# One 25-way switch for every two experts in place of a five-way switch for each expert

## The chip, the cores and the metric

The kernel runs on one core of a Trainium2 chip. Its engines are TensorE (PE, with its weight loads as PEld), VectorE (DVE), ScalarE (ACT), GpSimd (POOL) and SyncE (SP), which here issues nearly all DMAs. Each engine has its own program and its own sequencer. The metric is the time of one execution on the device in microseconds (us), as the median of several runs; a profile of one execution explains it.

## The reference

A trunk of two layers over 256 latent tokens and 256 context tokens of width 1024. Layer 0 is a bidirectional RWKV-7 mixer and a dense SwiGLU; layer 1 is a pooling mixer and a top-2-of-8 expert SwiGLU. All is in fp32. The change touches the last part alone:

```python
def swiglu(h, w1, w3, w2):
    return (jax.nn.silu(h @ w1) * (h @ w3)) @ w2

def moe_swiglu(h, router_w, router_b, w1, w3, w2):
    logits = (h @ router_w).astype(jnp.float32) + router_b.astype(jnp.float32)
    top_logit, top_idx = lax.top_k(logits, TOP_K)
    top_p = jax.nn.softmax(top_logit, axis=-1)
    gates = jnp.einsum('btk,btke->bte', top_p,
                       jax.nn.one_hot(top_idx, N_EXPERTS, dtype=jnp.float32)).astype(h.dtype)
    y = jnp.zeros_like(h)
    for e in range(N_EXPERTS):
        y = y + gates[..., e:e + 1] * swiglu(h, w1[e], w3[e], w2[e])
    return y
```

256 tokens with two experts each are 512 rows of work over 8 experts. How many rows an expert gets is known only at run time.

## The kernel before

The expert stage is the last third of the kernel. The router (L1617 to L1640) makes, on VectorE with small matmuls, `sel` (which token takes which expert), `posm` (the position of a token among the rows of an expert) and `pc` (the rows of each expert). L1643 to L1648 compare `pc` with the four bounds 32, 64, 128, 192 and write `cnt`, one whole number from 0 to 4 for each expert. `values_load` (L1697) loads these numbers into registers of TensorE, VectorE, ScalarE and SyncE (`ARM_ENGINES`).

L1931 is the loop over the eight experts. For each expert, POOL writes the one-hot matrix `oh` of the next expert (L1657), and then the four engines enter a switch with five arms, each on its own, by one computed branch. The profile gives the instructions of the switch itself to L2071 (moves, register operations, `COMPARE_BRANCH`) and L1934 (a prefetch hint for the way out, the first instruction of an arm). At the end of an arm another branch leads back to the common path. The arms differ by the blocks of rows that they work on:

- `[Full, Full]` over 192 rows, `[Full, Small]` from 129 to 192, `[Full]` from 65 to 128, `[Small]` from 33 to 64, `[Tiny]` up to 32.
- `Full` splits each weight into two parts (ScalarE L1284 `wh`, VectorE L1285 `wl`) and multiplies in three passes (L237). `Small` and `Tiny` take the weights as they are (L1786 and L1800; L1751 and L1769), with column groups of TensorE for several pieces at once.

`arm(e, kinds)` (L1858) goes through one expert in a fixed order of 13 steps, "u0 u1 u2 d0 u3 d1 ... t5 d4 d5": u is the up product, t a turn (L1763 in Tiny, L1832 in Full), d the down product. In the step t5 it already gathers the tokens of the next expert: `gather(oh, xgs[0])` (TensorE L1666, then VectorE L1653 and ScalarE L1652 write `xg`), `halves()` splits them (L1674, L1675), `turn_oh` turns the one-hot (L1681). At the end of the arm VectorE writes the expert's output rows to `yf` (L1775 in Tiny, L1850 in Full). The next expert's arm adds them to the sum: `scatter` (TensorE L1724, VectorE L1726). A Full arm does this scatter first of all, a Tiny or Small one after its step u1.

The weights come in 17 pieces of an expert, mostly 1 MB each, over SyncE's queue (L1536). 19 slots in SBUF hold them; when a step has used a piece, SyncE starts the load of the piece 19 further on in the same slot.

Instructions within one straight block are put in order by a scheduler that may move work of a later step ahead; between the blocks of a switch nothing moves. POOL is not part of the switch.

Of the kernel before, what the change touches and what calls it, by code (L numbers as in the profile page):

```python
# [8 lines left out]
F32 = mybir.dt.float32  # L9
F32R = mybir.dt.float32r  # L10
I32 = mybir.dt.int32
AF = mybir.ActivationFunctionType
ALU = mybir.AluOpType
# [4 lines left out]
P = 128  # L18
# [7 lines left out]
NE = 8  # L26
BOUNDS = (32, 64, 128, 192)
# [71 lines left out]
class Sched:  # L99
# [12 lines left out]
    def op(self, tag, fn, deps=(), acq=(), use=(), at=0.0, nbytes=0, dur=None):  # L112
        o = Op()
        o.tag, o.fn, o.acq, o.nbytes = tag, fn, list(acq), nbytes
        o.eng, us, rank = WORK[tag]
        o.dur, o.prio = us if dur is None else dur, at + rank
        for t in acq:
            t.by = o
        deps = [d for d in deps if d is not None] + [t.by for t in use if t.by is not o]
        o.wait, o.ready, o.end, o.next, o.seq, o.names = len(deps), 0.0, None, [], len(self.ops), None  # L120
        for d in deps:
            d.next.append(o)
        for t in list(acq) + list(use):
            t.users.append(o)
        self.ops.append(o)
        return o
# [74 lines left out]
def kernel(ctx: ExitStack, tc: tile.TileContext, I: dict, out: bass.AP, dbg=None):  # L201
    nc = tc.nc
# [55 lines left out]
    def ada_copy(ps):  # L258
        nc.vector.tensor_copy(ab, ps[:, 0:256])

    def ada_turn(pt):
        for j in range(2):
            nc.tensor.transpose(pt[:, P * j:P * j + P], ab[:, P * j:P * j + P], ident)
# [331 lines left out]
    S = Sched()  # L595
# [9 lines left out]
    def tok(n):  # L605
        return rings[n].tok()
# [7 lines left out]
    def pb(t):  # L614
        return PB[t.i + (2 if t.ring is rings["gen"] else 0)]
# [35 lines left out]
    for q in range(4):  # L651
# [7 lines left out]
        for h in range(2):  # L659
# [6 lines left out]
            a = op("v_hi", v_hi, deps=[ld], acq=[sp[h]], use=[rw], at=-1.5 + 0.5 * q)  # L666
# [12 lines left out]
        for tp in range(2):  # L679
# [8 lines left out]
            a = op("v_out", v_out, deps=prev[2 * tp:2 * tp + 2] + [opened], acq=[vt], use=[accs[tp]], at=-1.5 + 0.5 * q)  # L688
# [6 lines left out]
    for n, (l, w) in enumerate(todo[ada_at[0]:]):  # L695
# [14 lines left out]
        a = op("ada_copy", lambda: ada_copy(ADAB), deps=mms + ada_done[-1:], use=[bt], at=pr)  # L710
        g = tok("gen")
        t = op("ada_turn", lambda g=g: ada_turn(pb(g)), deps=[a], acq=[g], at=pr)
# [553 lines left out]
    c2p = ctx.enter_context(tc.tile_pool(name="c2p", bufs=1, reuse_waits="tile"))  # L1266
# [54 lines left out]
    def C2(n, a=0, b=None):  # L1321
        o, w = CONST2[n]
        return consts2[:, o - POOLED + a:o - POOLED + (w if b is None else b)]
# [206 lines left out]
    def piece(g):  # L1530
        sh = pieces[g][1]
        return slots[g % NS][:, 0:math.prod(sh[1:])].rearrange("p (a b) -> p a b", a=sh[1])
# [70 lines left out]
    exp_p = ctx.enter_context(tc.tile_pool(name="exp_p", bufs=1, reuse_waits="tile"))  # L1603
# [31 lines left out]
    pp, pc = gen(), gen()  # L1635
    pe(nc.tensor.matmul(pp[:, 0:16], lhsT=C2("tri"), rhs=sel.rearrange("p t e -> p (t e)"), start=True, stop=False))
    pe(nc.tensor.matmul(pp[:, 8:16], lhsT=C2("ones"), rhs=sel[:, 0], start=False, stop=True))
    for t in range(2):
        pe(nc.tensor.matmul(pc[:, 0:8], lhsT=C2("ones"), rhs=sel[:, t], start=(t == 0), stop=(t == 1)))
    nc.vector.scalar_tensor_tensor(posm, sel, -1000.0, pp[:, 0:16].rearrange("p (t e) -> p t e", t=2),  # L1640
                                   op0=ALU.mult, op1=ALU.add)

    cnt = c2p.tile([P, NE], I32, name="cnt")  # L1643
    armf = c2p.tile([P, NE], F32, name="armf")
    S.chain(nc.vector.tensor_scalar(armf, pc[:, 0:8], float(BOUNDS[0]), None, op0=ALU.is_le))
    for i, b in enumerate(BOUNDS[1:]):
        S.chain(nc.vector.scalar_tensor_tensor(armf if i + 2 < len(BOUNDS) else cnt, pc[:, 0:8], float(b), armf,
                                               op0=ALU.is_le, op1=ALU.add))  # L1648
    ENG = mybir.EngineType
    def affine3(dt, dst, src):  # L1650
        if dt % 2:
            return nc.scalar.activation(dst, src, AF.Identity, scale=r_a[:, dt:dt + 1], bias=r_b[:, dt:dt + 1])  # L1652
        return nc.vector.tensor_scalar(dst, src, r_a[:, dt:dt + 1], r_b[:, dt:dt + 1], op0=ALU.mult, op1=ALU.add)  # L1653

    def onehot(e, b, eng, oh):
        for t in range(2):
            eng.tensor_scalar(oh[:, t], C2("iota", P * b, P * b + P), posm[:, t, e:e + 1], None, op0=ALU.is_equal)  # L1657

    def gather(oh, xg, n=P):

        for d4 in range(2):
            pt = gen()
            for j in range(4):
                dt = 4 * d4 + j
                for t in range(2):
                    nc.tensor.matmul(pt[:, P * j:P * j + n], lhsT=z[:, t, P * dt:P * dt + P], rhs=oh[:, t, 0:n], start=(t == 0), stop=(t == 1))  # L1666
            for j in range(4):
                affine3(4 * d4 + j, xg[:, 4 * d4 + j], pt[:, P * j:P * j + n])
# [8 lines left out]
    def turn_oh(oh, ohT):  # L1677

        po = gen()
        for t in range(2):  # L1680
            nc.tensor.transpose(po[:, P * t:P * t + P], oh[:, t], ident)  # L1681
        nc.scalar.activation(ohT, po[:, 0:256].rearrange("p (t s) -> p t s", t=2), AF.Copy)
# [4 lines left out]
    spare = sct.rearrange("p d c -> p (d c)")  # L1687
# [2 lines left out]
    xs3 = [exp_p.tile([P, DT, P], F32R, name="xs" + n) for n in "hl"]  # L1690
    yf = exp_p.tile([P, D], F32, name="yf")
    nc.gpsimd.memset(yf, 0.0)
    oh, ohB = exp_p.tile([P, 2, P], F32, name="oh"), spare.rearrange("p (t s) -> p t s", t=2)
    xgs = [exp_p.tile([P, DT, P], F32, name="xg"), None]
    ohT = [consts[:, 2 * P:4 * P].rearrange("p (t s) -> p t s", t=2), C2("tri", 0, 2 * P).rearrange("p (t s) -> p t s", t=2)]
    ARM_ENGINES = (ENG.PE, ENG.DVE, ENG.Activation, ENG.SP)
    vals = [nc.values_load(cnt[0:1, e:e + 1], engines=ARM_ENGINES, min_val=0, max_val=len(BOUNDS)) for e in range(NE)]  # L1697
    onehot(0, 0, nc.vector, oh)
    gather(oh, xgs[0])
    turn_oh(oh, ohT[0])  # L1700
    halves()
    ex, p1_, sm = rt("ex", [P, 2, 1]), rt("p1_", [P, 2, 1]), rt("sm", [P, 2, 1])
    nc.vector.tensor_tensor(ex, m2, m1, op=ALU.subtract)
# [148 lines left out]
    def rows_of(v):  # L1852
        return lambda k: v[k // v[0].shape[1]][:, k % v[0].shape[1]]
# [4 lines left out]
    def arm(e, kinds):  # L1858
        full, two, end = kinds[0] is Full, len(kinds) > 1, e == NE - 1
        if full and e > 0:  # L1860
            scatter(e - 1, ohT[(e - 1) % 2])
        if two:
            onehot(e, 1, nc.vector, ohB)
            n = P if kinds[1] is Full else 64
            xgs[1] = yf[:, 0:DT * n].rearrange("p (d s) -> p d s", d=DT)
            gather(ohB, xgs[1], n)
            turn_oh(ohB, ohT[(e + 1) % 2])
        w, at, g = {}, {}, 17 * e
        for a, c in acts:
            if a != "t":  # L1870
                at[a, c] = range(g, g + (2 if a == "u" and c < 5 else 1))
                g = at[a, c][-1] + 1
                w[a, c] = [piece(i) for i in at[a, c]]
                if a == "d":
                    w[a, c] = w[a, c][0]
                else:
                    w[a, c] = rows_of(w[a, c])
        bl = [k(w, xgs[b], b, accb[2 * ((e + b) % 2):2 * ((e + b) % 2) + 2]) for b, k in enumerate(kinds)]
        ups, dns = {}, {}
        eats = list(at)  # L1880

        def split(i):

            if not full or i >= len(eats):
                return
            a, c = eats[i]
            if a == "u":
                v = [piece(g) for g in at[a, c]]
                ups[c] = parts_of([split_weight(t) for t in v], v[0].shape[1])
            else:  # L1890
                dns[c] = split_weight(w["d", c])

        split(0)
        for a, c in acts:
            if a != "t":
                split(eats.index((a, c)) + 1)
            for k in bl[::-1]:
                if a == "u":
                    k.up(c, ups)
                elif a == "d":  # L1900
                    k.down(c, dns)
                else:
                    k.turn(c)
            if a == "u":
                for k in bl[::-1]:
                    if c > 0:
                        k.turn(c - 1)
                    k.act(c)
            if (a, c) == ("u", 1) and e > 0 and not full:
                scatter(e - 1, ohT[(e - 1) % 2])  # L1910
            if a == "t" and not end:
                gather(oh, xgs[0])
                halves()
                if not two:
                    turn_oh(oh, ohT[(e + 1) % 2])
            for i in at.get((a, c), ()):
                pload(i + NS)
        if two:
            bl[1].end()
            scatter(e, ohT[(e + 1) % 2])  # L1920
            if not end:
                turn_oh(oh, ohT[(e + 1) % 2])
        bl[0].end()

    ARMS = [[Full, Full], [Full, Small], [Full], [Small], [Tiny]]

    extra = ctx.enter_context(tc.tile_pool(name="extra", bufs=1, reuse_waits="tile"))
    for g in range(EXTRA):
        slots.append(extra.tile([P, 2048], F32, name=f"slot{MORE + g}"))
        pload(len(slots) - 1)  # L1930
    for e in range(NE):  # L1931
        if e + 1 < NE:
            onehot(e + 1, 0, nc.gpsimd, oh)
        for k in tc.Switch({g: vals[e] for g in ARM_ENGINES}, len(ARMS)):  # L1934
            arm(e, ARMS[k])
    scatter(NE - 1, ohT[(NE - 1) % 2])
    rg, rb = (piece(17 * NE + i)[:, 0] for i in range(2))
    z = zx.tile([P, 2, D], F32, tag="z", name="z4")
# [136 lines left out]
```

## Time and profile before

| | before |
|---|---|
| median of 3 runs (lowest to highest) | 1416.85 us (1416.37 to 1421.95) |
| profiled execution, its time | 1420.72 us |
| its span, first to last instruction | 1418.9 us |
| granted clock of TensorE, mean | 0.889 |
| busy: PE, DVE, ACT, POOL | 81%, 65%, 44%, 24% of the span |
| expert stage | about 943 to 1403 us |
| HBM read | 273.17 MB |

A row of the chain of waits has a start, a length and the engine, DMA or "issue" that the chain went through; "issue" is time in which an engine waited for nothing that the profile shows. A row of the timeline has a start, a length, engine, line, operation, output and inputs, shape and count, and in brackets the idle time before it with what ended it. A group with q behind the engine belongs to its sequencer (branches, register loads, DMA issues) and is not counted as busy time.

### The profile page before, as it was taken

The page shows a single profiled execution, that of the slowest core. Times are in us where ns is not written, and L with a number is a line of the kernel's source. Part 1 is how long each engine was busy: PE and PEld are TensorE (multiplying, and loading weights), DVE is VectorE, ACT ScalarE, POOL GpSimd, SP SyncE. Part 2 cuts the span into 40 slices and gives each one's busy share as a digit, 9 for nine tenths or more (in the row PEclk, how much of TensorE's full clock was granted, in tenths as well). Part 3 has the DMA queues.
Part 4 walks back from the last instruction along what each step waited for, and adds up shares of the span by engine and source line. Part 5 has one row for each costly group of instructions (what it writes and reads, how often), then busy time and mean ns, then how long its engine had stood idle before and what let it go on. Part 6 is the DMA issues. An engine that isn't in the chain of part 4 may idle for free.

```text
span 1418.9 us, 25963 instructions
## 1 busy us (share of the span) xinstructions
PE 1147.9 (81%) x9897; PEld 880.9 (62%) x9897; DVE 925.3 (65%) x1841; ACT 630.1 (44%) x1350; POOL 344.6 (24%) x467
## 2 busy tenths in 40 slices
PE   1589659977788788688699999957979899877885
PEld 0267448956566566554489898854768556554673
DVE  7797417857876776664967777661969655522865
ACT  3343218467555674222144444321858444311750
POOL 6341130037705667010622232040000000000000
PEclk8699779988977799589799999979999999999998
DMA  8225545566646446362934455739969445599960
GB/s 354 90 89 193 195 143 176 162 175 188 175 106 198 109 131 174 68 204 94 372 139 179 164 187 201 288 137 407 347 220 352 155 162 178 176 410 413 372 217 32
DMA packets 131598, 288.43 MB, mean 203 GB/s; under 512 B 63536, under 2 KB 90288, under 8 KB 108208
## 3 DMA queue, kind: packets, MB, share of 16 engines
q1 hardware_dynamic: 128064, 278.50, 56.2%
q10 hardware_dynamic: 3312, 7.31, 1.4%
q8 instruction: 98, 1.61, 0.5%
q14 instruction: 124, 1.02, 0.3%
HBM read 273.17 MB, written 12.60 MB: 201 GB/s over the span
## 4 chain that ended last, share of the span: by engine, by line
PE 37%; DVE 6%; issue 5%; DMA 4%; ACT 2%; SPq 0%; DVEq 0%; POOL 0%; ACTq 0%; POOLq 0%
PE pb L237 24%; PE pb L1751 3%; PE pb L1666 2%; PE pb L1786 2%; PE pb L1769 1%; DVE wl L1285 1%; DMA bpool<-in_consts_dram 1%; PE pb L1724 1%; DMA arena<-in_ffn_w_dram 1%; ACT wh L1284 1%; PE pb L1800 1%; DMA slot<-in_moe_w_dram 1%; DMA rows<-in_lnrows_dram 1%; DVE usl L1434 1%; DMA arena<-in_lnrows_dram 0%
## 5 line engine op out<-in xcount | busy, mean ns | idle before, releaser
L1285 DVE TENSOR_TENSOR wl<-arena,wh 128x512 fp32r<-128x512 f32 x266 | 213.2, 827 | 88.6 <-ACT wh L1284 75.5
L1284 ACT ACTIVATE wh<-arena 128x512 fp32r<-128x512 f32 x266 | 162.0, 628 | 135.9 <-PE pb L237 100.1
L237 PE MATMUL pb<-usl,wh 128*128 128x256 f32 x352 | 101.7, 289 | 12.6 <-DVE usl L1434 12.6
L1285 DVE TENSOR_TENSOR wl<-slot,wh 128x512 fp32r<-128x512 f32 x130 | 84.5, 686 | 38.8 <-ACT wh L1284 29.8
L1284 ACT ACTIVATE wh<-slot 128x512 fp32r<-128x512 f32 x130 | 79.3, 628 | 59.0 <-PE pb L237 28.9
L237 PE MATMUL pb<-ush,wl 128*128 128x256 f32 x352 | 100.8, 287 | 1.8 <-DVE wl L1285 1.8
L237 PE MATMUL pb<-ush,wh 128*128 128x256 f32 x352 | 100.7, 288 | 1.8 <-DVE fsg L1452 1.8
L1657 POOL TENSOR_SCALAR oh<-consts,consts 128x128 f32<-128x128 f32 x14 | 9.1, 659 | 351.9 <-PE pb L237 242.9
L1097 DVE SCALAR_TENSOR_TENSOR sv<-sv,wc,pb 64x64 f32<-64x64 f32 x192 | 45.8, 278 | 57.1 <-issue 23.7
L237 PE MATMUL pb<-wh,xsh 128*128 128x512 f32 (+1 forms) x192 | 74.6, 394 | 10.0 <-DVE x L1726 10.0
L237 PEld LDWEIGHTS pb<-usl,wh 128*128 128x128 f32 x352 | 68.9, 196 | 16.2 <-DVE usl L1434 14.0
L1072 ACT ACTIVATE sv<-pb 64x128 f32<-64x128 f32 x128 | 34.5, 270 | 100.0 <-PE pb L1066 94.5
L1316 POOL TENSOR_TENSOR arena<-arena,rows 128x2048 f32<-128x2048 f32 x11 | 52.5, 4786 | 104.2 <-DMA arena<-in_ffn_w_dram 104.2
L237 PE MATMUL pb<-wl,xsh 128*128 128x512 f32 (+1 forms) x192 | 76.2, 397 | 0.0
L237 PE MATMUL pb<-wh,xsl 128*128 128x512 f32 (+1 forms) x192 | 73.1, 381 | 0.0
L944 POOL TENSOR_TENSOR arena<-arena 128x56 f32<-128x56 f32 (+22 forms) x155 | 69.6, 449 | 12.1
L237 PEld LDWEIGHTS pb<-ush,wh 128*128 128x128 f32 x352 | 68.5, 196 | 4.1 <-DVE fsg L1452 2.0
L237 PEld LDWEIGHTS pb<-ush,wl 128*128 128x128 f32 x352 | 69.0, 196 | 3.2 <-DVE wl L1285 2.0
L1724 PE MATMUL pb<-yf,consts 128*128 128x512 f32 x72 | 42.7, 735 | 28.3 <-issue 26.9
L1759 DVE TENSOR_TENSOR mh<-mh,pb 64x128 f32<-64x128 f32 (+1 forms) x24 | 7.0, 291 | 82.9 <-ACT mh L1758 43.7
L853 PE MATMUL pb<-arena 128*128 128x192 f32 x256 | 53.7, 363 | 5.3 <-DVE slotsw L869 2.0
L853 PEld LDWEIGHTS pb<-arena 128*128 128x128 f32 x256 | 46.2, 209 | 10.4 <-DVE slotsw L869 2.7
(442 smaller groups left out, 3084.0 us busy)
## 6 DMA issues: line engine op xcount, KB each, us to landing
slot<-in_moe_w_dram SPq DMA_DIRECT2D x62, 1024.0 KB, 10.3
arena<-in_moe_w_dram SPq DMA_DIRECT2D x58, 1024.0 KB, 5.9
arena<-in_ffn_w_dram SPq DMA_DIRECT2D x33, 1024.0 KB, 4.8
arena<-in_ada_w_dram SPq DMA_DIRECT2D x28, 512.0 KB, 4.2
ada<-in_ada_w_dram SPq DMA_DIRECT2D x28, 512.0 KB, 4.2
hvr<-in_w_rkv_dram SPq DMA_DIRECT2D x12, 1024.0 KB, 16.0
wr<-in_ada_w_dram SPq DMA_DIRECT2D x10, 1024.0 KB, 4.8
sv<-v_d SPq DMA_DIRECT2D x128, 64.0 KB, 3.5
```

The costliest lines, as they stand in the source:

```text
L237: i = nc.tensor.matmul(ps, lhsT=a[x], rhs=b[y], start=start and n == 0, stop=stop and n == 2)
L853: nc.tensor.matmul(pb(g)[:, 192 * j:192 * j + 192], lhsT=kap_b[kap.i][:, c + j].rearrange("p h t -> p (h t)"), rhs=kbi_b[kbi.i][:, c + j])
L944: eng.tensor_tensor(T[:, cs, ii], T[:, cs, ii], mv, op=ALU.subtract)
L1072: nc.scalar.activation(sv_(si, d, 1)[zd(d)], bank[zd(d), 0:128], AF.Copy, scale=-1.0)
L1097: nc.vector.scalar_tensor_tensor(t[:, x], sv_(si, d, 0)[zd(d), x], wc_b[wc.i][zd(d), h, si:si + 1], bank[zd(d), 128 + 64 * h:192 + 64 * h] ...
L1284: nc.scalar.activation(hi, r[:, o:o + PART], AF.Copy)
L1285: nc.vector.tensor_tensor(lo, r[:, o:o + PART], hi, op=ALU.subtract)
L1316: S.behind(nc.gpsimd.tensor_tensor(w, w, gt.unsqueeze(1).to_broadcast(w.shape), op=ALU.mult))
L1666: nc.tensor.matmul(pt[:, P * j:P * j + n], lhsT=z[:, t, P * dt:P * dt + P], rhs=oh[:, t, 0:n], start=(t == 0), stop=(t == 1))
L1724: nc.tensor.matmul(ps, lhsT=ohT[:, t], rhs=yf[:, 512 * j:512 * j + 512], start=True, stop=True)
L1751: nc.tensor.matmul(ps[32 * g:32 * g + 32, 0:P], lhsT=xg[:, k, 0:32], rhs=m[g], start=(k == 0), stop=(k == DT - 1))
L1786: nc.tensor.matmul(ps[64 * g:64 * g + 64, 0:n], lhsT=xg[:, k, 0:64], rhs=m[g], start=(k == 0), stop=(k == DT - 1))
```

## The change

Eight switches become four. Each covers the experts e and e + 1 and has 25 arms, one for each pair of cases, so that the two experts of a pair stand in one straight block. `cnt` holds four numbers, 5 times the case of the first expert plus that of the second, made by one operation more on VectorE. There are two one-hot buffers in place of one; POOL fills both ahead of a switch, for the experts e + 1 and e + 2.

```diff
-    cnt = c2p.tile([P, NE], I32, name="cnt")
+    cnt = c2p.tile([P, NE // 2], I32, name="cnt")
     armf = c2p.tile([P, NE], F32, name="armf")
     S.chain(nc.vector.tensor_scalar(armf, pc[:, 0:8], float(BOUNDS[0]), None, op0=ALU.is_le))
-    for i, b in enumerate(BOUNDS[1:]):
-        S.chain(nc.vector.scalar_tensor_tensor(armf if i + 2 < len(BOUNDS) else cnt, pc[:, 0:8], float(b), armf,
-                                               op0=ALU.is_le, op1=ALU.add))
+    for b in BOUNDS[1:]:
+        S.chain(nc.vector.scalar_tensor_tensor(armf, pc[:, 0:8], float(b), armf, op0=ALU.is_le, op1=ALU.add))
+    pairs = armf.rearrange("p (a b) -> p a b", b=2)
+    S.chain(nc.vector.scalar_tensor_tensor(cnt, pairs[:, :, 0], float(len(BOUNDS) + 1), pairs[:, :, 1], op0=ALU.mult, op1=ALU.add))
...
-    oh, ohB = exp_p.tile([P, 2, P], F32, name="oh"), spare.rearrange("p (t s) -> p t s", t=2)
+    ohs, ohB = [exp_p.tile([P, 2, P], F32, name=f"oh{i}") for i in range(2)], spare.rearrange("p (t s) -> p t s", t=2)
...
-    vals = [nc.values_load(cnt[0:1, e:e + 1], engines=ARM_ENGINES, min_val=0, max_val=len(BOUNDS)) for e in range(NE)]
-    onehot(0, 0, nc.vector, oh)
-    gather(oh, xgs[0])
-    turn_oh(oh, ohT[0])
+    vals = [nc.values_load(cnt[0:1, i:i + 1], engines=ARM_ENGINES, min_val=0, max_val=(len(BOUNDS) + 1) ** 2 - 1)
+            for i in range(NE // 2)]
+    onehot(0, 0, nc.vector, ohs[0])
+    gather(ohs[0], xgs[0])
+    turn_oh(ohs[0], ohT[0])
...
             if a == "t" and not end:
+                oh = ohs[(e + 1) % 2]
                 gather(oh, xgs[0])
...
-    for e in range(NE):
-        if e + 1 < NE:
-            onehot(e + 1, 0, nc.gpsimd, oh)
-        for k in tc.Switch({g: vals[e] for g in ARM_ENGINES}, len(ARMS)):
-            arm(e, ARMS[k])
+    for e in range(0, NE, 2):
+        for i in range(e + 1, min(e + 3, NE)):
+            onehot(i, 0, nc.gpsimd, ohs[i % 2])
+        for k in tc.Switch({g: vals[e // 2] for g in ARM_ENGINES}, len(ARMS) ** 2):
+            arm(e, ARMS[k // len(ARMS)])
+            arm(e + 1, ARMS[k % len(ARMS)])
```

## The prediction

> **What bounds the kernel now.** I began with the page's chain of work that ended last, for the shares of the whole span, and then had the chain listed in order of time for the expert stage alone (960 to 1403 us).
>
> ```profile
> PE 37%; DVE 6%; issue 5%; DMA 4%; ACT 2%; SPq 0%; DVEq 0%; POOL 0%; ACTq 0%; POOLq 0%
> ```
>
> ```profile
> 979.90 6.06 issue
> 986.56 6.26 issue
> ...
> 1051.01 4.15 issue
> 1055.80 3.69 issue
> ...
> 1114.54 4.36 issue
> 1119.55 3.65 issue
> ...
> 1225.76 8.03 DMA slot<-in_moe_w_dram
> ...
> 1265.26 4.46 issue
> 1270.37 6.08 issue
> ...
> 1301.64 6.30 issue
> 1308.53 6.65 issue
> ...
> 1370.49 5.54 DMA arena<-in_lnrows_dram
> ```
>
> The columns are start, length and what held the chain. "issue" is 5% of 1418.9 us, and these rows show where most of it lies: seven places, 5.5 to 13 us each, at the seven borders between experts. A border has two issue rows because an engine leaves one arm (first row) and then enters the next (second row). Two borders, 1225.76 and 1370.49, are put down to a DMA instead; I take that for a label, since TensorE's own branch covers the same time, as the next view shows. I asked for the branch instructions, one border at a time (PEldq is TensorE's sequencer; minimum, median and maximum in ns, then the start):
>
> ```profile
> L2071 PEldq COMPARE_BRANCH  x1: 7239/7239/7239, 979.4 to 979.4; - x1
> ...
> L2071 PEldq COMPARE_BRANCH  x1: 5905/5905/5905, 1113.7 to 1113.7; - x1
> ...
> L2071 PEldq COMPARE_BRANCH  x1: 6706/6706/6706, 1226.9 to 1226.9; - x1
> ...
> L2071 PEldq COMPARE_BRANCH  x1: 6725/6725/6725, 1262.4 to 1262.4; - x1
> ...
> L2071 PEldq COMPARE_BRANCH  x1: 5365/5365/5365, 1371.7 to 1371.7; - x1
> ```
>
> One branch occupies TensorE's sequencer for 5.4 to 7.2 us. The DMA queues between 979 and 987 us say why:
>
> ```profile
> q8 instruction: 2, 0.03, 2.7%
> ```
>
> (Queue, kind, packets, MB, share.) Two packets of program code, 0.03 MB, are fetched in that gap on a queue that carries nothing else: I read the branch as waiting for the code it jumps to. The seven borders follow experts 0 to 6. The shapes in the timeline give the arms that this input takes: Tiny, Full, Full, Full+Small, Tiny, Tiny, Full, Tiny.
>
> **The change, part by part.** The new switch runs experts (0,1), (2,3), (4,5), (6,7) in one arm each. So the borders 0-1, 2-3, 4-5 and 6-7 become straight code, and the borders 1-2, 3-4, 5-6 and the entry keep a branch. I price each removed border by the first instruction that can start sooner.
>
> Border 0-1, Tiny to Full:
>
> ```profile
> 978.90 0.61 PE L1769 MATMUL pb<-slot,consts 128*32 128x256 f32 x8
> 986.88 5.91 PE L1724 MATMUL pb<-yf,consts 128*128 128x512 f32 x8 [7.37 <-issue]
> 996.59 0.77 PE L237 MATMUL pb<-wh,xsh 128*128 128x512 f32 x1 [3.80 <-DVE x L1726]
> ...
> 979.69 1.77 DVE L1775 TENSOR_TENSOR yf<-pb,gt 32x256 f32<-32x256 f32 x4 [0.38 <-PE pb L1769]
> ...
> 993.05 2.19 ACT L1284 ACTIVATE wh<-slot 128x512 fp32r<-128x512 f32 x4 [12.59 <-PE pb L1724]
> ...
> 1402.27 3.70 PE L1724 MATMUL pb<-yf,consts 128*128 128x512 f32 x8 [1.46 <-DVE yf L1775]
> ...
> 997.00:1002.00 5.00, 5.00 (x14) 0.54 0.88 340
> 1002.00:1049.00 47.00, 47.00 (x241) 1.00 0.88 326
> ```
>
> The scatter of expert 0 (L1724) needs yf, done at 979.69 + 1.77 = 981.46. Eight scatter matmuls take 3.70 us at full clock (the row at 1402.27; here 5.91 at the low clock). So without branches the first split matmul of expert 1 can start at about 981.5 + 4.0 = 985.5 in place of 996.59: 11.1 us. ScalarE and VectorE are free to split the first weights before that, since their late start (993.05) is the same branch. The clock stands in the last two rows (after the busy time: granted clock, DMA share, GB/s): 0.54 for 5 us after the gap, then 1.00. The first 5 us run at about half speed, so about 2.3 us of work are lost there; with TensorE idle for 2 us instead of two long gaps I expect none of that. **Together 13.4 us.**
>
> Border 2-3, Full to Full+Small:
>
> ```profile
> 1112.92 0.39 PE L237 MATMUL pb<-wh,hh1l 128*128 128x512 f32 x1
> 1119.84 5.99 PE L1724 MATMUL pb<-yf,consts 128*128 128x512 f32 x8 [6.53 <-issue]
> 1126.28 1.89 PE L1666 MATMUL pb<-sct,z 128*128 128x64 f32 x15 [0.45 <-DVE x L1726]
> ...
> 1113.86 0.68 DVE L1850 TENSOR_TENSOR yf<-pb,gt 128x512 f32<-128x512 f32 x1
> ```
>
> The second half of yf is done at 1114.54, the scatter takes 3.7 to 4.0 us, so the gather for the second block starts near 1118.6 in place of 1126.28: **7.7 us**.
>
> Border 4-5, Tiny to Tiny:
>
> ```profile
> 1262.03 0.61 PE L1769 MATMUL pb<-arena,consts 128*32 128x256 f32 x8
> 1269.56 6.36 PE L1751 MATMUL pb<-slot,xg 128*32 128x128 f32 x128 [6.92 <-DMA arena<-in_moe_w13b_dram]
> 1276.94 0.27 PE L1763 MATMUL pb<-consts,mh 64*128 64x64 f32 x1 [1.02 <-DVE mh L1759]
> ...
> 1244.23 1.95 PE L1751 MATMUL pb<-slot,xg 128*32 128x128 f32 x64
> ```
>
> The tokens xg are already gathered in the arm of expert 4, so the 128 up matmuls can follow at about 1263. At full clock they take 2 x 1.95 = 3.9 us, and the turn (L1763) comes at 1266.9 in place of 1276.94: 10.0 us. I take off 1 us, because the up matmuls at 1269.56 took 1.2 us longer than those at 1377.57 below, and a wait for weights or code may remain: **9.0 us**.
>
> Border 6-7, Full to Tiny:
>
> ```profile
> 1377.57 5.12 PE L1751 MATMUL pb<-arena,xg 128*32 128x128 f32 x128 [6.21 <-issue]
> 1382.62 0.27 PE L1763 MATMUL pb<-consts,mh 64*128 64x64 f32 x1
> ```
>
> The gap of 6.21 us before the first row began at 1371.37. From there 128 up matmuls at full clock end at 1375.3, so the turn comes 7.2 us sooner: **7.2 us**.
>
> The four are 37.3 us. The chain's own rows at these borders (12.3, 8.0, 10.5 and 5.5) make 36.3 us and support it by another way.
>
> The kept borders. At 1-2 the chain goes through VectorE, which spends 4.15 us leaving the arm and 3.69 us entering. A longer arm may make its exit cheaper: at border 3-4, after the longest arm, no such row is in the chain. TensorE waited there only 0.9 us for VectorE, so I count a gain of 0.9 us (nearest to that wait); 4 us is the upper bound, and 4 us lost the lower one, if an exit that is cheap now becomes as dear as VectorE's here.
>
> The table in VectorE (L1645 to L1647) gets a fifth operation ahead of the first one-hot, which TensorE waits for:
>
> ```profile
> 942.76 0.36 DVE L1647 SCALAR_TENSOR_TENSOR armf<-pb,armf 128x8 f32<-128x8 f32 x2
> ```
>
> That is 0.2 us a step: plus 0.2 us. SyncE loads four values in place of eight before the first switch; its next weights come about 2 us sooner, but 19 slots hold more than the 17 pieces of an expert and nothing waits for them then: 0. The one-hots of two experts are now made together on POOL at the start of a pair. TensorE first needs one of them in the gather at the end of the first expert, over 20 us later; without that cover it would cost about 1.2 us a pair, the time of one one-hot. The second buffer exists so that POOL need not wait for the gather. The jump itself I take as no dearer with 25 targets: each dispatch is one branch record, not a row of comparisons.
>
> Do weights arrive in time? Through experts 4 and 5 the DMA engines are full:
>
> ```profile
> 1277.00:1301.00 24.00, 22.25 (x360) 15.42 (x360) 6.62 (x14) 4.82 (x16) 0.02 (x1) 1.00 1.01 417
> ...
> 1319.00:1371.00 52.00, 51.96 (x255) 43.62 (x255) 47.34 (x84) 42.84 (x81) 0.00 (x0) 0.97 0.90 339
> ```
>
> (Length, busy us of PE, weight loads, DVE, ACT and POOL, then clock, DMA share, GB/s; the second row is a Full arm, for rival (a).) At 417 GB/s a piece of 1 MB takes 2.5 us, so the 15 or 16 pieces of expert 5 that do not fit ahead land about 41 us after expert 4 starts. It starts at 1226.9 + 6.7 = 1233.6, and expert 5 is left at 1301.6: 68 us, in the new order 59. About 18 us of cover are left of 27; if it is gone, up to the 9.0 us of border 4-5 come back.
>
> **Sum:** 37.3 + 0.9 - 0.2 = 38.0 us. Against the profiled execution (1420.7 us, of which 1418.9 are the span) this gives 1382.7; the median of the shown runs is 3.9 us lower, and 1416.85 - 38.0 = **1379 us**.
>
> **The rivals.** (a) Only TensorE's idle time goes. If the merged arm is ordered so that VectorE still splits and adds late, and the clock dips anyway, what is left is 986.88 - 981.5, 1119.84 - 1114.54, 1269.56 - 1263.0 and 6.2: 23.5 us, 1393 us. For it: in a Full arm VectorE is busy 47.34 of 52 us, so it has little room to catch up. Against it: in a Tiny arm it is busy 6.62 of 24, and can split the next expert's first weights there. (b) More goes. If leaving the pair (4,5) also gets cheap for ScalarE (6.30 us in the chain at 1301.64; TensorE waits 5.3 us there later) and border 1-2 gives 4 us, the time is 1371 us. Against it: leaving short arms is what is slow on ScalarE now. (c) The gaps are not the branches' own. The branch records would then be waits for something that remains, and the time is about 1416. The Trainium skill speaks for this: Advanced Engine Details and Errata, Control Flow Timing, puts a branch at about 51 ns and a compare-and-branch at about 108 ns, by which four borders with two branches each would give back under 1 us (an estimate from that page). The trace does not agree: 7239 ns in one record, with code packets beside it. (d) Slower. The 25 arms make the program about five times as long, and each jump goes further. If a jump into it costs more, the place is the four dispatches that remain; it decides once each costs 38 / 4 = 9.5 us more than now. At 12 us more (leaving plus entering at 979.90, 6.06 + 6.26, once again) the time is 1379 + 48 = 1427 us. Against it: each fetch lies between 5.4 and 7.2 us whether the target is the third or the last arm.
>
> **How the numbers follow.** Forecast 0.56, (a) 0.22, (b) 0.12, (c) 0.05, (d) 0.05. The range 1366 to 1396 covers the forecast, (a) and (b) with about 3 us beyond, and leaves out (c) and (d). About 0.5%, 7 us, is what a measurement can tell from no change. Faster by more: 0.56 + 0.22 + 0.12 = 0.90; within it: 0.05; slower: 0.05.
>
> **What would show it.** Right: four dispatch records on TensorE in place of eight; at 0-1 a wait for yf of about 2 us and then a scatter of about 4 us at full clock; the first split matmul of expert 1 about 6 us after the last matmul of expert 0 (now 17). Wrong: dispatch records well over 7 us, a new TensorE wait for a weight DMA in expert 5, or waits for VectorE in the first 10 us of experts 1 and 3.

## The result

Four runs of the changed kernel took 1382.31 us at the median (1379.28 to 1389.20), four of the kernel before 1418.88 us (1416.37 to 1421.95): a ratio of 0.9748 (95% interval 0.9703 to 0.9793). The forecast was 1379 in a range of 1366 to 1396. The profiled execution was the longest of the four, 1389.2 us, of which 1387.3 are the span.

In the changed kernel the line numbers of the expert stage are 1 to 5 higher (L1724 is now L1726, L1769 is L1771, L2071 is L2076). In what follows a jump is the branch into an arm; its length is that of the record on TensorE, and on the other engines, whose record is short, the time from the record to the first instruction of the arm. The way out runs from an engine's last work in an arm to its next register load. The planner is the scheduler that puts the instructions of a block in order.

The page of the changed kernel, queues and chain (queue, kind, packets, MB, share of 16 engines; then the shares of the chain that ended last):

```profile
q8 instruction: 87, 1.43, 0.4%
q14 instruction: 80, 0.66, 0.2%
...
PE 37%; DMA 7%; DVE 5%; issue 2%; ACT 1%; SPq 0%; POOL 0%; DVEq 0%; POOLq 0%; ACTq 0%
```

"issue" fell from 5% to 2% of the chain, while TensorE's share stayed. Less program code is fetched although the program is longer.

The branch instructions on TensorE's sequencer that take over 1 us, one border at a time (minimum, median, maximum in ns, then the start):

```profile
L2076 PEldq COMPARE_BRANCH  x1: 6833/6833/6833, 951.5 to 951.5; - x1
...
L2076 PEldq COMPARE_BRANCH  x1: 5733/5733/5733, 1043.6 to 1043.6; - x1
...
L2076 PEldq COMPARE_BRANCH  x1: 7964/7964/7964, 1209.9 to 1209.9; - x1
...
L2076 PEldq COMPARE_BRANCH  x1: 6781/6781/6781, 1274.5 to 1274.5; - x1
```

Four jumps are left of eight: the entry and the borders 1-2, 3-4, 5-6. The timeline of TensorE and VectorE at the removed borders 0-1, 2-3 and 4-5:

```profile
987.47 0.61 PE L1771 MATMUL pb<-slot,consts 128*32 128x256 f32 x8
988.28 1.77 DVE L1777 TENSOR_TENSOR yf<-pb,gt 32x256 f32<-32x256 f32 x4 [0.40 <-PE pb L1771]
989.20 3.70 PE L1726 MATMUL pb<-yf,consts 128*128 128x512 f32 x8 [1.12 <-DVE yf L1777]
992.34 0.80 PE L237 MATMUL pb<-wh,xsh 128*128 128x512 f32 x1
...
1105.75 3.70 PE L1726 MATMUL pb<-yf,consts 128*128 128x512 f32 x8 [0.36 <-DVE yf L1852]
...
1246.45 0.61 PE L1771 MATMUL pb<-arena,consts 128*32 128x256 f32 x8
1246.88 3.68 PE L1753 MATMUL pb<-slot,xg 128*32 128x128 f32 x128
```

At 0-1 TensorE waits 1.12 us for yf, makes the scatter in 3.70 us at full clock, and starts expert 1 at 992.34, 4.3 us after expert 0's last matmul (17.1 before). At 4-5 the up matmuls of expert 5 follow with no gap at all, and 128 of them take 3.68 us where 6.36 were needed after the branch.

Where the time went, from the two timelines and once more from the second profile of the changed kernel (the run "again" below). Each row is TensorE's time from the last matmul of one part to the last of the next; minus is a gain. The row that ends with expert 7 runs to the start of the last scatter, and the rest from there to the end of the span:

| stretch | before, us | after | again | change | forecast |
|---|---|---|---|---|---|
| entry: router's first matmul to expert 0's first up matmul | 12.7 | 14.7 | 15.0 | +2.0, +2.3 | +0.2 |
| expert 0 | 26.2 | 29.3 | 27.5 | +3.1, +1.3 | 0 |
| border 0-1 and expert 1 | 70.3 | 55.3 | 55.3 | -14.9, -15.0 | -13.4 |
| 1-2 to the end of expert 3 | 178.8 | 168.2 | 168.9 | -10.6, -9.9 | -8.6 |
| 3-4 to the end of expert 5 | 72.7 | 63.1 | 60.8 | -9.6, -11.9 | -9.0 |
| 5-6 to the end of expert 7 | 101.0 | 95.2 | 96.3 | -5.8, -4.7 | -7.2 |
| rest | 16.7 | 17.4 | 16.5 | +0.7, -0.2 | 0 |
| sum | 478.3 | 443.2 | 440.2 | -35.1, -38.1 | -38.0 |

What lies ahead of this stage is the same work in both kernels and ended between 937 and 951 us in the profiles of this study. For that reason I compare profiles by the stage alone: from the router's first matmul (L1636) to the end of the span.

The kept border 3-4 with expert 4 is inside a row: it took 1.4 us more than before in one profile and 1.0 less in the other, while 4-5 with expert 5 gave 11.0 in both.

### The profile page after: what moved, and what is told of

It is laid out like the page before. It is cut to its first block, busy times and chain, and to the rows that moved or that the text cites. A ratio compares the mean times of both kernels' runs of the same rounds, so it can differ in the third digit from the quotient of the medians.

```text
span 1387.3 us, 25795 instructions
## 1 busy us (share of the span) xinstructions
PE 1145.4 (83%) x9897; PEld 879.9 (63%) x9897; DVE 927.3 (67%) x1842; ACT 630.0 (45%) x1350; POOL 344.4 (25%) x467
## 4 chain that ended last, share of the span: by engine, by line
PE 37%; DMA 7%; DVE 5%; issue 2%; ACT 1%; SPq 0%; POOL 0%; DVEq 0%; POOLq 0%; ACTq 0%
PE pb L237 25%; DMA slot<-in_moe_w_dram 3%; PE pb L1753 3%; PE pb L1726 2%; PE pb L1667 2%; PE pb L1788 2%; DMA bpool<-in_consts_dram 1%; DMA arena<-in_moe_w_dram 1%; DVE wl L1285 1%; PE pb L1771 1%; DMA arena<-in_ffn_w_dram 1%; PE pb L1802 1%; ACT wh L1284 1%; DMA rows<-in_lnrows_dram 1%; DVE usl L1434 1%
## 5 line engine op out<-in xcount | busy, mean ns | idle before, releaser
L1284 ACT ACTIVATE wh<-arena 128x512 fp32r<-128x512 f32 x266 | 162.4, 628 | 139.4 <-PE pb L237 119.3
L1284 ACT ACTIVATE wh<-slot 128x512 fp32r<-128x512 f32 x130 | 79.3, 628 | 41.0 <-PE pb L237 27.2
L944 POOL TENSOR_TENSOR arena<-arena 128x56 f32<-128x56 f32 (+22 forms) x155 | 72.7, 469 | 12.2
L237 PE MATMUL pb<-wh,xsl 128*128 128x512 f32 (+1 forms) x192 | 72.2, 376 | 0.0
L1346 POOL TENSOR_TENSOR rs_y<-rs_v,mhalf 128x1 f32<-128x1 f32 x8 | 5.2, 660 | 195.3 <-DVE rs_v L1345 195.3
L853 PEld LDWEIGHTS pb<-arena 128*128 128x128 f32 x256 | 45.8, 208 | 11.3 <-DVE slotsw L869 2.9
L1726 PE MATMUL pb<-yf,consts 128*128 128x512 f32 x72 | 39.4, 683 | 16.1 <-issue 13.1
```

The lines of the kernel that those rows point to most:

```text
L237: i = nc.tensor.matmul(ps, lhsT=a[x], rhs=b[y], start=start and n == 0, stop=stop and n == 2)
L853: nc.tensor.matmul(pb(g)[:, 192 * j:192 * j + 192], lhsT=kap_b[kap.i][:, c + j].rearrange("p h t -> p (h t)"), rhs=kbi_b[kbi.i][:, c + j])
L944: eng.tensor_tensor(T[:, cs, ii], T[:, cs, ii], mv, op=ALU.subtract)
L1284: nc.scalar.activation(hi, r[:, o:o + PART], AF.Copy)
L1726: nc.tensor.matmul(ps, lhsT=ohT[:, t], rhs=yf[:, 512 * j:512 * j + 512], start=True, stop=True)
```

## The experiments

Theory A is the forecast's: each border costs the branch's own way out, jump and start, so a border that is straight code gives that back. Against it stood B (the second one-hot buffer did it), C (a longer program makes jumps dearer, the gain is net of that) and D (the gain is the planner's freedom to interleave two experts in one block).

**The buffers alone.**

```diff
+            if a == "t" and not end:
+                oh = ohs[(e + 1) % 2]
...
+        for i in range(e + 1, min(e + 3, NE)) if e % 2 == 0 else ():
+            onehot(i, 0, nc.gpsimd, ohs[i % 2])
         for k in tc.Switch({g: vals[e] for g in ARM_ENGINES}, len(ARMS)):
```

> The kernel before with its eight five-way switches; of the change only the two one-hot buffers and the one-hots written for two experts at once. Theory A (each border costs its own way out, jump and start): 1416 to 1420, no change from before, 8 jump records, border 0-1 still about 17 us. Theory B (the gain came from the second buffer, which lets the next expert's gather be made without waiting): most of the 36 us gain, 1380 to 1395.

Measured 1422.76 against 1422.69 us for the kernel before, ratio 1.0006 (0.9984 to 1.0028). The stage took 477.1 us. Border 0-1 in its timeline:

```profile
984.47 1.19 PE L1724 MATMUL pb<-yf,consts 128*128 128x512 f32 x1 [7.34 <-issue]
```

The gap of 7.3 us is untouched. B falls.

**Twenty-five arms, eight switches.**

```diff
-        for k in tc.Switch({g: vals[e] for g in ARM_ENGINES}, len(ARMS)):
-            arm(e, ARMS[k])
+        for k in tc.Switch({g: vals[e] for g in ARM_ENGINES}, 25):
+            arm(e, ARMS[min(k, 4)])
```

> The kernel before with eight switches, each of 25 arms; arms 5 to 24 are never taken and are copies of the Tiny arm, so that the program behind the switches is about five times as long. Theory A: jump and way out do not depend on the number of arms: 1412 to 1424, jump records 5.4 to 7.5 us as before. Theory C (a jump into a longer program is dearer, and the gain of the change is net of that): each of eight jumps 1 to 3 us dearer, 1425 to 1440. The way out of an arm that was the last one (Tiny) and is so no more may be dearer on SyncE.

Measured 1426.36 us, ratio 1.003 (1.0005 to 1.0055), at the edge of what can be told. Two of its eight jumps:

```profile
L2071 PEldq COMPARE_BRANCH  x1: 4859/4859/4859, 950.4 to 950.4; - x1
...
L2071 PEldq COMPARE_BRANCH  x1: 7126/7126/7126, 1228.6 to 1228.6; - x1
```

The eight jump records sum to 49.0 us; in the kernel before they sum to 49.2. The stage took 478.8 us against 478.3. So neither 25 arms nor a longer program behind the switches makes a jump dearer, and C and rival (d) of the prediction fall so far as this kernel tests them: the arms that it takes are still the first five of each switch, and the added ones are copies of the shortest arm. In the kernels with these four pairs in 25 arms, two of TensorE's jumps were dearer than in the four kernels with eight switches: at 1-2 5.7 to 6.8 us against 5.6, at 3-4 7.1 to 8.0 against 6.2 to 7.1. Why is open. The 0.3% was not placed.

**Other pairs.** Expert 0 alone, (1,2), (3,4), (5,6), expert 7 alone:

```diff
+    for i, es in enumerate(((0,), (1, 2), (3, 4), (5, 6), (7,))):
...
+        for k in tc.Switch({g: vals[i] for g in ARM_ENGINES}, len(ARMS) ** len(es)):
+            for n, e in enumerate(es):
+                arm(e, ARMS[k // len(ARMS) ** (len(es) - 1 - n) % len(ARMS)])
```

> The changed kernel with the pairs moved by one: expert 0 alone, (1,2), (3,4), (5,6), expert 7 alone; five switches. Theory A: borders 1-2, 3-4, 5-6 lose their gaps (about 12.7 to 4, 5.5 to 0, 17.8 to 4: 28 us in sum) and 0-1, 2-3, 4-5, 6-7 get theirs back: 1385 to 1395 by the gaps of the kernel before; the border 0-1 is 16 to 18 us again. Theory B (buffers and freedom of order over the whole stage): about the same as the changed kernel, 1375 to 1385, with no gap that comes back.

Measured 1406.40 us, ratio 0.9884 (0.9836 to 0.9931). The places follow A: the border 0-1 has its gap again, and 1-2 has lost its own.

```profile
990.98 1.19 PE L1728 MATMUL pb<-yf,consts 128*128 128x512 f32 x1 [6.98 <-issue]
...
1054.32 1.98 PE L1728 MATMUL pb<-yf,consts 128*128 128x512 f32 x4 [0.36 <-DVE yf L1854]
...
1272.14 2.19 ACT L1284 ACTIVATE wh<-arena 128x512 fp32r<-128x512 f32 x4 [16.32 <-DMA arena<-in_moe_w_dram]
1274.36 0.27 ACT L1762 ACTIVATE mh<-pb 64x128 f32<-64x128 f32 x1
...
1275.74 0.37 PE L1767 MATMUL pb<-consts,mh 64*128 64x64 f32 x1 [5.67 <-DVE mh L1763]
```

The size does not: 11 us were missing to the nearer end of A's numbers. Border 1-2 gave 9.0 us with its two experts, as expected; 3-4 gave 3.2 in place of 5.5, 5-6 gave 11.3 in place of 13.8, the gap at 4-5 grew by 2.4 and the entry by 2.2. The last three rows show one reason. In the pair (5,6) the planner put ScalarE's splitting of expert 6's first weights (L1284) ahead of expert 5's first activation (L1762). Those weights had not landed, ScalarE stood for 16.32 us, and TensorE waited 5.67 us for a product that was otherwise ready to be made. So D is wrong as the source of the gain, but the planner's freedom can cost part of it.

**A fence inside the arm.** On each engine every instruction of the first expert ahead of every one of the second:

```diff
             arm(e, ARMS[k // len(ARMS)])
...
+            for on in (nc.tensor, nc.vector, nc.scalar, nc.sync):
+                f = on.nop()
...
             arm(e + 1, ARMS[k % len(ARMS)])
+            for q in list(nc.cur_bb.bb.instructions)[n1:]:
+                tc.add_manual_dep(q, fence[q.engine], S.same, reason="order")
```

> The changed kernel with, on each engine, every instruction of the pair's first expert ahead of every one of its second. No instruction may move across the border inside an arm, but there is no branch there. Theory A: within 6 us of the changed kernel, 1378 to 1388; the borders 0-1 and 2-3 stay at 4 to 5 us. Theory D (the gain is the planner's, which may interleave two experts once they stand in one block): most of the gain goes, 1400 to 1415.

Measured 1380.95 us, ratio 0.9691 (0.9640 to 0.9742). Border 0-1:

```profile
985.09 1.13 PE L1726 MATMUL pb<-yf,consts 128*128 128x512 f32 x2 [1.09 <-DVE yf L1777]
```

The whole gain stays without any motion across the border inside a pair: D falls. The stage took 436.7 us, the shortest of the paired kernels; the kernel's time cannot be told from the changed one.

**No switch at all.**

```diff
...
-        for k in tc.Switch({g: vals[e // 2] for g in ARM_ENGINES}, len(ARMS) ** 2):
+        for k in ((22, 11, 24, 14)[e // 2],):
```

> The changed kernel with the four switches left out: the code of the four arms that this input takes stands in one straight line, so the choice by the counts of the run is left out. Theory A (what is left at the three kept borders and at the entry is the branches' own): entry -5 to -6 us, border 1-2 -7.5, 3-4 -6, 5-6 -12.5 against the changed kernel, 1350 (1343 to 1358), and no PE gap over 2 us at a border. Theory D (the planner gets more freedom than it can use, and puts the next expert's weights ahead of the running one on ScalarE and VectorE, as was seen at one place with the pairs moved by one): a wait of 4 to 6 us for activations in one or two experts, 1355 to 1370.

Measured 1349.60 us, ratio 0.9508 (0.9471 to 0.9545); the stage 407.3 us. TensorE in expert 0 and at border 1-2, which has no jump now:

```profile
954.15 5.61 PE L1751 MATMUL pb<-arena,xg 128*32 128x128 f32 x136 [3.59 <-ACT xg L1653]
...
1032.96 3.70 PE L1724 MATMUL pb<-yf,consts 128*128 128x512 f32 x8 [0.35 <-DVE yf L1850]
```

The three borders and the entry that the change keeps cost another 33 us at the medians, which is A's sum, and no gap over 2 us is left at a border. The places do not all follow A, so that the sum met it to the microsecond is in part luck. Against the first profile of the changed kernel the entry gave 6.1 us (5 to 6 expected), but TensorE then waited 3.59 us for the gathered tokens `xg` in expert 0; border 1-2 with expert 2 gave 7.2 (7.5), 3-4 with experts 3 and 4 only 2.9 (6), and the stretch from border 5-6 to the last scatter 14.9 (12.5). The remaining 4.9 us lie in experts 0, 1 and 5 and the rest. This kernel serves this input only, so it is a bound and not a version to use.

**Early hints.** First for the first switch on four engines and for later ones on VectorE and ScalarE, then for the first switch on TensorE alone. The edit of the second:

```diff
+    tc.switch_hint({ENG.PE: vals[0]}, 25, "group0")
     onehot(0, 0, nc.vector, ohs[0])
```

> The changed kernel with early prefetch hints for jumps: for the first switch on all four engines ahead of the gather of expert 0; for the later switches on VectorE and ScalarE at the start of the second expert of a pair that takes a short arm, where it takes the place of the hint for the way out, which missed there anyway. Theory A (a jump is dear because the code behind it has not been fetched): the first jump falls from 5 to 7 us to under 2, since the gather's 5 us lie behind the hint, and the 5.2 us for which TensorE waits for VectorE after border 5-6 shrink to under 1.5: 1371 to 1377. Rival (the cost is the jump's own, or hints only act when the engine runs on into new code): 1380 to 1385, first jump 5 to 7 us.

Measured 1390.31 us, ratio 0.9760 (0.9716 to 0.9805): not faster than the changed kernel. TensorE's first jump fell to 2.4 us, and TensorE then waited 7.6 us for VectorE. The hints for the later switch missed: after border 5-6 VectorE's way out still took 4.6 us and TensorE still waited 3.2 us for it (5.2 and 4.0 in the two profiles without hints).

> The changed kernel with one early prefetch hint, on TensorE alone, for the first switch, ahead of expert 0's gather; VectorE and ScalarE are left as they were. Theory A (the jump waits for code to be fetched, and the hint starts that fetch): TensorE's first jump 2 to 3 us in the place of 5 to 7, expert 0's first up matmul 3 to 4 us earlier, and 2 to 3 us of it kept to the end: 1378 to 1381. Rival (the value has to be there before the gather, so the gather waits for it): the gather starts 1 to 2 us later and the gain is under 1 us: 1381 to 1384.

Measured 1387.69 us, ratio 0.9750 (0.9722 to 0.9778), beside 0.9732 (0.9700 to 0.9765) for the unaltered changed kernel on the same chip. The first jump and the timeline behind it, with the hint on TensorE alone:

```profile
L2077 PEldq COMPARE_BRANCH  x1: 2421/2421/2421, 955.8 to 955.8; - x1
```

```profile
958.64 4.02 PE L1754 MATMUL pb<-arena,xg 128*32 128x128 f32 x125 [0.26 <-issue]
...
967.03 2.19 ACT L1284 ACTIVATE wh<-slot 128x512 fp32r<-128x512 f32 x4 [5.92 <-issue]
...
971.24 0.37 PE L1766 MATMUL pb<-consts,mh 64*128 64x64 f32 x1 [7.77 <-DVE mh L1762]
```

On TensorE the expected mechanism shows, and the gain does not come. TensorE's jump fell from 6.8 to 2.4 us, and its up matmuls began 6.7 us after the first gather matmul (11.5 before the hint). But ScalarE and VectorE now took 5.7 and 5.3 us for their own jumps, where both needed 2.9, and TensorE then waited 7.77 us for them. Those jumps now fell where DMA was busy 0.56 and 0.54 of the time, in place of 0.23 and 0.08. In the first of the two kernels, hints given 10 us ahead on ScalarE and VectorE did not shorten their first jumps either (6.5 and 5.9 us). So TensorE's jump behaves like a wait for code that has to be fetched; on ScalarE and VectorE no hint showed that. On which engine the wait ends last decides what a hint is worth.

**A longer arm on VectorE.** The kernel before with 24 one-element additions in each arm that is Full alone:

```diff
...
+            if full and a == "u":
+                for _ in range(4):
+                    nc.vector.tensor_scalar(pad, pad, 1.0, None, op0=ALU.add)
```

> The kernel before with 24 additions of one element per partition on VectorE in every arm that is Full alone, so that such an arm has 139 to 142 instructions on VectorE in the place of 115 to 117. Theory (an engine's way out of an arm is cheap where the arm was long enough, over about 128 instructions, for the code behind it to be fetched): VectorE's way out at borders 1-2, 2-3 and 6-7 falls from 4 to 5.5 us to under 1.5, as it is after expert 3 with 142; at 0-1, 4-5 and 5-6 (28 to 31 instructions) it stays. The time changes little, since TensorE's own jump ends later there: 1412 to 1424. Rival (the way out depends on the border, not on the arm's length): no change at any border.

One run: 1420.39 us, not to be told from 1421.48 for the kernel before. VectorE's way out (last work to the next register load) went from 4.15, 4.36 and 3.75 us at borders 1-2, 2-3 and 6-7 to nothing at all three; at 0-1, 4-5 and 5-6 it stayed at 4.0 to 4.6. So on VectorE the length of the arm decides. VectorE at border 1-2, kernel before:

```profile
1050.33 0.68 DVE L1850 TENSOR_TENSOR yf<-pb,gt 128x512 f32<-128x512 f32 x1
...
1059.74 1.89 DVE L1285 TENSOR_TENSOR wl<-slot,wh 128x512 fp32r<-128x512 f32 x3 [8.73 <-issue]
```

and with the longer arm:

```profile
1049.40 0.68 DVE L1852 TENSOR_TENSOR yf<-pb,gt 128x512 f32<-128x512 f32 x1
1055.83 0.53 DVE L1915 TENSOR_SCALAR pad<-pad 128x1 f32<-128x1 f32 x3 [5.74 <-issue]
```

The idle time fell by 3.0 us, less than the way out, since the jump itself was then longer (5.6 us against 3.7).

**The changed kernel again.**

> The changed kernel once more, unaltered. In its first profile the entry (router's first matmul to expert 0's first up matmul) took 2.0 us and expert 0 itself 3.1 us more than before. If that belongs to the change, entry 14 to 15 us and expert 0 29 us again; if it belonged to that execution, 12.5 to 13.5 and 26 to 27, and a span of about 1380 to 1383. Time 1379 to 1385 either way.

Measured 1384.19 us, ratio 0.9732 (0.9700 to 0.9765). The entry was 15.0 us once more, so that loss belongs to the change; expert 0 took 27.5 us, so of its 3.1 us more than half was that execution's. Expert 0 took 24.1 to 26.2 us in the four kernels with eight switches, so it varies by itself. TensorE's first jump:

```profile
L2076 PEldq COMPARE_BRANCH  x1: 6993/6993/6993, 955.4 to 955.4; - x1
```

**SyncE later.** TensorE's first jump record took 4.8 to 5.3 us in the four kernels with eight values to load and 5.8 to 7.0 in five with fewer. With fewer loads SyncE makes its own jump first (950.6 against TensorE's 951.5; before, 949.4 against 948.0). So:

```diff
+    late = [nc.values_load(cnt[0:1, i:i + 1], engines=(ENG.SP,), min_val=0, max_val=24) for i in range(4)]
```

> The changed kernel with four more loads of a count into a register on SyncE ahead of the first switch, so eight as in the kernel before: SyncE starts its first jump some 2 us later. In the four kernels with eight loads the stretch from expert 0's first gather matmul to its first up matmul took 9.7 to 9.9 us with a first jump of TensorE of 4.9 to 5.4; in the five kernels with three to five loads and no early hint 10.6 to 11.9 with 5.8 to 7.0. Theory (SyncE now jumps first, and TensorE's code is fetched behind SyncE's): the stretch falls back under 10.2 and the jump under 5.5, and 2 to 4 us of it stay to the end: 1379 to 1382. Rival (the longer first arms, not SyncE's order): 11 to 12 us with a jump of 6 to 7 again, 1382 to 1386.

Measured 1380.32 us, ratio 0.9704 (0.9669 to 0.9739).

```profile
L2077 PEldq COMPARE_BRANCH  x1: 5013/5013/5013, 944.3 to 944.3; - x1
...
L2077 SPq COMPARE_BRANCH  x1: 43/43/43, 945.4 to 945.4; - x1
```

The jump is back at 5.0 us, the stretch from the first gather matmul to the first up matmul at 9.9 (11.5 and 11.9 without the delay), and expert 0 at 25.6. Entry and expert 0 together took 38.6 us: 37.0 to 38.9 in the four kernels with eight loads, 39.9 to 43.9 in the five with fewer and no early hint. So it is the earlier start of SyncE that had made TensorE's jump dearer. The stage took 438.7 us against 443.2 and 440.2; at the medians the gain cannot be told from none.

**Larger groups.** (0,1), (2,3,4), (5,6,7), with four cases for each expert, without and with the hint on TensorE. Of the same groups with all five cases (25, 125 and 125 arms) there is no measurement. The edit, in part:

```diff
+    for i, es in enumerate(((0, 1), (2, 3, 4), (5, 6, 7))):
...
-BOUNDS = (32, 64, 128, 192)
+BOUNDS = (32, 128, 192)
```

> Groups (0,1), (2,3,4), (5,6,7), three switches, with four cases for each expert (the case up to 64 tokens is left out: such an expert would take the one up to 128; none has that case here), so 16, 64 and 64 arms. Borders 3-4 and 5-6 go, 4-5 comes back, with an arm long enough for a cheap way out. Theory A: against the changed kernel -6 (3-4), -12.5 (5-6), +9 (4-5): 1373 (1368 to 1379), jumps 5.5 to 8 us. Theory D (the planner's order inside a longer block makes a new wait, as with the pairs moved by one): 1378 to 1385.

Measured 1382.99 us, ratio 0.9720 (0.9689 to 0.9751).

> The two before in one: three groups with four cases, and the early hint on TensorE for the first switch. Theory A: sum of both, 1370 (1365 to 1376). Rival: as the groups alone, 1373 to 1379.

Measured 1389.69 us, ratio 0.9771 (0.9737 to 0.9806). One switch fewer, and no gain. The first of the two, border 4-5:

```profile
1252.73 6.05 PE L1756 MATMUL pb<-slot,xg 128*32 128x128 f32 x128 [9.76 <-DMA arena<-in_moe_w_dram]
1259.93 2.19 ACT L1284 ACTIVATE wh<-arena 128x512 fp32r<-128x512 f32 x4 [16.00 <-DMA arena<-in_moe_w_dram]
1262.14 0.27 ACT L1763 ACTIVATE mh<-pb 64x128 f32<-64x128 f32 x1
1263.52 0.37 PE L1768 MATMUL pb<-consts,mh 64*128 64x64 f32 x1 [4.74 <-DVE mh L1764]
```

The returned border 4-5 cost 18.1 us with expert 5, not 9: a gap of 9.76 us, up matmuls at the low clock, and again ScalarE held by the next expert's weights (16.00 us, TensorE 4.74). At 3-4 the removed gap was 6.8 us, yet from the restart after border 1-2 to the end of expert 4 only 2.2 us were won against the first profile of the changed kernel, and nothing against the second. There the planner pushed expert 4's narrow up matmuls between the wide ones of expert 3:

```profile
1206.49 0.40 PE L237 MATMUL pb<-wh,hh0l 128*128 128x512 f32 x1
1206.82 0.41 PE L1756 MATMUL pb<-slot,xg 128*32 128x128 f32 x4
1207.16 0.50 PE L237 MATMUL pb<-wl,hh0h 128*128 128x512 f32 x1
```

A wide matmul that follows another starts 0.23 us after it; around the four narrow ones 0.67 us pass. There are 12 such places with 50 narrow matmuls, and 9.0 us pass there from wide to wide; 12 wide steps and 50 narrow matmuls in a row (at the 3.70 us for 128 that the fence shows at border 6-7) would make about 4.2. So the interleaving took about 4.8 us, by this estimate; no run left it out here. The kernel without switches and the pairs moved by one have the same 12 places, so the same loss stands in their 3-4.

## Why the prediction was right, step by step

**What bounds the kernel at a border** was right: the gaps are the branches'. Buffers alone change nothing, the fence keeps the gain, straight code leaves no gap at a border, and the pairs moved by one move the gaps.

**Border 0-1** was right in mechanism and a little low: 14.9 us with expert 1 against 13.4. The wait for yf was 1.12 us where I put 2, since the first yf half is enough to start the scatter; and 50 us of expert 1 ran at a clock of 1.00 from its start:

```profile
993.00:998.00 5.00, 5.00 (x23) 4.11 (x22) 4.38 (x7) 4.04 (x7) 0.00 (x0) 1.00 1.02 418
998.00:1043.00 45.00, 45.00 (x232) 38.02 (x231) 41.25 (x75) 38.74 (x75) 3.28 (x4) 1.00 1.01 415
```

**Border 2-3** gave 9.0 us with expert 3, 7.7 forecast, and **4-5** gave 11.0 with expert 5, 9.0 forecast, both the same in two profiles. The microsecond taken off there for a wait for weights or code was not needed.

**Border 6-7** was over-sized, and by the planner's order. The stretch from border 5-6 on gave 4.7 to 5.8 us where 7.2 were forecast, but it also holds the restart after the kept border 5-6: the first 5 us of expert 6 ran at a granted clock of 0.70 and 0.50 in the two profiles. From the 41st split matmul of expert 6 to the last scatter that is over, and there the runs agree: 72.2 to 72.4 us in all five kernels that have a jump at 6-7, 67.0 in both profiles of the changed kernel (5.2 gained), 64.5 with the fence (7.7 gained). In the changed kernel 72 up matmuls of expert 7 stand between expert 6's last matmuls; with the fence none does, and they come in one row:

```profile
1340.52 3.70 PE L1753 MATMUL pb<-arena,xg 128*32 128x128 f32 x128
```

So the border itself gives what was forecast, and the order across it takes 2.5 us back. The five places where the 72 stand account for about 1.5 of that; the rest of the order was not separated.

**Kept borders.** VectorE's way out of 1-2 became cheap, as weighed, and the border with expert 2 gave 1.6 and 0.9 us in the two profiles (0.9 forecast). The experiment with the longer arm shows the cause that the forecast only guessed.

**SyncE at nothing** was a wrong step. I looked at what SyncE's earlier loads would do for its weights and not at what its earlier jump would do to TensorE's. The entry lost 2.0 to 2.3 us where 0.2 were forecast, and with SyncE delayed it was back at 13.0 us in one profile. Expert 0 after it lost 1.3 to 3.1 and was back too, but the spread of expert 0 among the kernels with eight switches is 2 us, so how much of that is SyncE's is open. That the two engines' code shares one path is the likeliest reading, not shown directly.

**The jump as no dearer** held at border 5-6 (6.7 us before, 6.8 in both profiles after) and not quite at 1-2 (5.6 before, 5.7 and 6.2 after) and 3-4 (6.7 before, 8.0 and 7.1 after). By the forecast's own list of signs, a record well over 7 us was a sign of being wrong; it came at 3-4 in the first profile, and that border with expert 4 lost 1.4 us in the first profile and gained 1.0 in the second.

**The sum** came out (38.0 forecast; 35.1 and 38.1 in two profiles) because the larger gains at 0-1, 2-3 and 4-5 paid for the entry, expert 0 and 6-7. That it came so close is in part luck: single places are off by 1 to 5 us.

**The rivals.** (a) fell at 0-1, where clock and idle time both came back. (b) fell: leaving the pair (4,5) is still dear. (c) fell with the straight kernel. The Trainium skill, Advanced Engine Details and Errata, Control Flow Timing, puts a compare-and-branch at about 108 ns. TensorE's jumps into an arm without an early hint are far from that, with 4.8 to 8.0 us, forty times as much and more; the measurement decides. (The records on ScalarE, VectorE and SyncE are under 0.1 us; there the time passes before the next instruction.) (d) fell with the result: no jump costs 9.5 us more.

## What to carry to other kernels

Price a switch by the jump into the arm, engine by engine: it held TensorE for 5 to 8 us here, with 5 targets as with 25, and 2.4 us after an early hint, which fits code that has to be fetched first; each other engine pays its own. Removing a border between two arms is worth what the first instruction that can then start gains, but a block that now holds two experts should be looked through for work of the second that stands ahead of the first's. And where several engines jump at one time, the order in which they do so can be part of the cost, as it was at the entry.

## What the runs showed that I had not expected

**A jump's length goes with the DMA traffic.** Over ten profiles without early hints, 30 jumps of ScalarE, VectorE and SyncE that fell where DMA was busy under 10% took 2.8 to 4.0 us (median 3.5); 65 that fell where it was over 90% took 5.1 to 7.3 (median 6.3). The 73 between took 2.6 to 7.9 (median 5.2), so the share alone does not set the length. VectorE in the changed kernel at the entry and at border 5-6, from jump to arrival (length first; the DMA share is the last figure but one):

```profile
956.80:959.70 2.90, 0.88 (x20) 0.91 (x24) 0.00 (x0) 0.68 (x2) 0.00 (x0) 0.57 0.08 23
1282.52:1288.93 6.41, 4.38 (x8) 1.58 (x6) 0.00 (x0) 0.51 (x1) 0.00 (x0) 0.81 1.02 408
```

TensorE's jumps fit less well: its first one, jump to arrival, took 4.9 to 5.4 us at a share of 0.94 and more where it led SyncE's. That the weights delay the code was not tried; no run changed the traffic alone.

**VectorE's way out of an arm is cheap from a certain length on.** Here some 117 instructions missed and some 141 hit, in the same arms, with nothing but padding to tell them apart. Where between them the limit lies was not tried.

**A hint is not a gain by itself.** It cut TensorE's first jump to 2.4 us, and the kernel was not faster.
